# Hybrid encoder layer: the gate rows of the dense tokens multiplied on VectorE instead of GpSimd, with staging buffers on two sides of SBUF and five block loads placed in one of them

## The chip, the core and the metric

One core of a Trainium2 chip runs the whole program. The metric is device time in microseconds (us); lower is better. Engines are named as the profile names them: PE is TensorE (PEld its weight loads), DVE is VectorE, ACT is ScalarE, POOL is GpSimd, SP is SyncE. SPq, ACTq and POOLq are the DMA issues of an engine.

## What is computed

One encoder layer over 1024 tokens of width 1024 in float32: RMSNorm and an input projection, differential attention and a two-way retention, an output projection, then a product-key expert layer (PEER), and a last RMSNorm. The change lies in the expert layer, for one block of tokens:

```python
q = (xb @ w_query).reshape(tb, 8, 2, 128)
s = einsum('thpd,hpnd->thpn', q, sub_keys)           # 8 heads, two halves, 128 keys each
top_s, top_i = top_k(s, 16)
cand_s, cand_i = all sums and pairs of the two halves  # 16 x 16 a head
best_s, pos = top_k(cand_s, 16)
eid  = take_along_axis(cand_i, pos)                  # 16 of 16384 experts a head, 128 a token
gate = softmax(best_s)
act  = gelu(einsum('thkd,td->thk', take(expert_down, eid), xb))
out  = einsum('thk,thkd->td', gate * act, take(expert_up, eid))
```

## The kernel before

The 1024 tokens are eight tiles of 128. Three of them (set A) are done by *gathering*: POOL fetches, for each of the 128 chosen experts of every token, one row of 1024 numbers from `peer_u` (128 tokens at a time, one indirect DMA into a tile called `rows`, six buffers), DVE multiplies it with the token's vector `xng` and sums into `act` (L998), and later the same is done with `peer_v` into `gacc` (L1007). That is 768 indirect DMAs in all.

The other five tiles (set B, 640 tokens, the *dense tokens*) are done *densely*: all 16384 experts, in 128 blocks of 128. For a block `a`, PE makes the products of the block of `peer_u` (the input `ut[a]`) with the tokens, ACT applies Gelu (`hf`, 128 experts x 640 tokens), and DVE multiplies by a block of gates that is zero where an expert was not chosen (`gt`, L1070). The product goes, as high and low halves `hh` and `hl`, into a second matmul with the block of `peer_v` (`po`), and DVE adds it up in `acc` (L1104). Each float32 factor is split in two halves (`uh` by ACT at L1060, `ul` by DVE at L1061; `vh` and `vl` likewise), and three matmuls make one product.

The gates come from a stage of their own, **the gates stage** (L902 to L940). For each of the five dense tiles, `kT` and `gT` hold the chosen keys and gates, turned so that a token is a column. Then, for every group of four tokens (32 groups a tile, 160 in all):

- DVE makes the one-hot patterns of both key halves, `oh` (L920);
- ACT converts the second half into `bo` (L924);
- POOL multiplies the first half by the gates into `ao` (L927); in three of 32 groups ACT does it in four pieces (L930);
- PE multiplies `bo` with `ao`, which gives a token's 128 x 128 gates, `pg` (L933);
- ACT, or in 13 of 32 groups DVE, copies `pg` into the staging tile `stg` (L936, L938), 64 KB a partition, two buffers in one pool.

After a tile, eight stores of 1 MB move `stg` to the DRAM tensor `g_dr` (L940). The last tile's stores end the stage.

Then comes **the prologue** of the dense loop (L1122 to L1145): the first five blocks of `ut` are loaded into five tiles `first0` to `first4` (L1125, on ACT's queue) in a pool that lies where `stg` lay. For each of the five, ACT and DVE split it, PE makes its products into `hfirst`, and four gathers are taken. After that, the gates of the five blocks are loaded from `g_dr` into the same `first` tiles (L1141), `acc` is loaded with x (L1143), and the five multiplies L1070 on `first` follow; with the first of them the second matmuls can begin. The loop over blocks 5 to 127 takes 6 gathers a block.

What sets the order: the code is written for a tile framework that gives every engine its own list of instructions, by a scheduler, and adds the waits. Each engine, and each DMA queue, works through its list in order. A tile in a pool that takes the room of a closed pool waits for what last used that room.

Lines that the prediction's steps touch:

```python
stg = pg_.tile([P, P, P], F32, name="stg")                                   # L917
G.tensor_tensor(ao, oh[0], bc(gT[:, q:q + 4, None], [P, 4, P]), op=ALU.mult)  # L927
first = [pp.tile([P, DC * P], F32, name=f"first{a}") for a in range(FIRST)]   # L1123
nc.sync.dma_start(gts[a], g_dr[a])                                            # L1141
mark[0] = V.tensor_tensor(gt, gt, hf, op=ALU.mult).ins                        # L1070
```

Of the kernel before, what the change touches and what calls it, by code (L numbers as in the profile page):

```python
# [10 lines left out]
F32 = mybir.dt.float32  # L11
# [4 lines left out]
AF = mybir.ActivationFunctionType  # L16
ALU = mybir.AluOpType
# [4 lines left out]
P = 128  # L22
# [3 lines left out]
DC = D // P  # L26
# [14 lines left out]
FIRST = 5  # L41
# [13 lines left out]
def peer_layer(tc, ap, dbg=None):  # L55
    nc = tc.nc
# [3 lines left out]
    def bc(a, shape):  # L60
        return a.to_broadcast(shape)
# [15 lines left out]
    with ExitStack() as top:  # L77
# [821 lines left out]


        g_dr = dram.tile([P, P, wB], F32, name="g_dr")
        with ExitStack() as es:  # L902
            pc = es.enter_context(tc.tile_pool(name="gc", bufs=1))
            pw = es.enter_context(tc.tile_pool(name="gw", bufs=4))
            pg_ = es.enter_context(tc.tile_pool(name="gs", bufs=2))
            ps = es.enter_context(tc.tile_pool(name="gps", bufs=2, space=PSUM))
            iop = pc.tile([P, P, 4], BF16, name="iop")
            G.iota(iop, pattern=[[1, P], [0, 4]], base=0, channel_multiplier=0, allow_small_or_imprecise_dtypes=True)
            for i in range(nB):
                pT = ps.tile([P, 3, P], F32, name="gtp")  # L910
                for k in range(3):
                    PE.transpose(pT[:, k], selE[k][:, i].rearrange("p h k -> p (h k)"), ident)
                kT = pw.tile([P, 2, P], BF16, name="kT", bufs=1)
                V.tensor_copy(kT, pT[:, 0:2])
                gT = pw.tile([P, P], F32, name="gT", bufs=1)
                V.tensor_copy(gT, pT[:, 2])
                stg = pg_.tile([P, P, P], F32, name="stg")  # L917
                for q in range(0, P, 4):
                    o2 = pw.tile([P, 2, P, 4], BF16, name="oh")
                    V.tensor_tensor(o2, bc(iop[:, None], [P, 2, P, 4]), bc(kT[:, :, None, q:q + 4], [P, 2, P, 4]),  # L920
                                    op=ALU.is_equal)
                    oh = [o2[:, k].rearrange("p n t -> p t n") for k in range(2)]
                    bo = pw.tile([P, 4, P], F32, name="bo")
                    S.activation(bo, oh[1], AF.Copy)  # L924
                    ao = pw.tile([P, 4, P], F32, name="ao")
                    if q // 4 % 11:
                        G.tensor_tensor(ao, oh[0], bc(gT[:, q:q + 4, None], [P, 4, P]), op=ALU.mult)  # L927
                    else:
                        for j in range(4):
                            S.activation(ao[:, j], oh[0][:, j], AF.Copy, scale=gT[:, q + j:q + j + 1])  # L930
                    pg = ps.tile([P, 4, P], F32, name="pg", bufs=6)
                    for j in range(4):
                        PE.matmul(pg[:, j], bo[:, j], ao[:, j], start=True, stop=True)  # L933
                    dst, src = stg[:, :, q:q + 4], pg.rearrange("p t a -> p a t")
                    if q // 4 % 5 in (0, 2):
                        V.tensor_copy(dst, src)  # L936
                    else:
                        S.activation(dst, src, AF.Copy)  # L938
                for k in range(0, P, 16):
                    nc.sync.dma_start(g_dr.rearrange("a b t -> b a t")[:, k:k + 16, i * P:(i + 1) * P], stg[:, k:k + 16])  # L940
        early.close()


        gp = top.enter_context(tc.tile_pool(name="gp", bufs=1, side="right"))
        late = {}

        def tail(t, o):
# [65 lines left out]
        with ExitStack() as es:  # L1013
# [105 lines left out]
                        add(k, t)  # L1119


            with tc.tile_pool(name="pro", bufs=1, side="right") as pp:  # L1122
                first = [pp.tile([P, DC * P], F32, name=f"first{a}") for a in range(FIRST)]  # L1123
                for a, ur in enumerate(first):
                    S.dma_start(ur.rearrange("p (c e) -> p c e", e=P), ap["ut"][a])  # L1125
                load(FIRST)
                for a, ur in enumerate(first):
                    raw[a] = ur.rearrange("p (c e) -> p c e", e=P)
                    split_u(a)
                    ready[a] = ready[a], pp.tile([P, wB], F32, name=f"hfirst{a}")  # L1130
                    products(ps, ready[a][1], 2, *ready[a][0])
                    ready[a] = ready[a][1]
                    for _ in range(4):
                        next(gen)
                split_u(FIRST)
                load(FIRST + 1)
                values(0)
                values(1)
                for a, ur in enumerate(first):
                    gts[a] = ur[:, 0:wB]  # L1140
                    nc.sync.dma_start(gts[a], g_dr[a])  # L1141
                for t, o in zip(SETS["B"], acc):
                    nc.sync.dma_start(o, x1_dr[t])  # L1143
                for a in range(FIRST):
                    down(a)  # L1145
            for a in range(FIRST - 1, P):
                if a >= FIRST:
                    down(a)
# [70 lines left out]
```

## Time and profile before

| | |
|---|---|
| median of three runs | 3086.2 us (3084.46 to 3092.26) |
| the profiled run, its own time | 3082.46 us |
| span of the profiled run, first to last instruction | 3080.7 us |
| PE busy | 2830.5 us (92%) |
| DVE busy | 2556.9 us (83%) |
| POOL busy | 1678.9 us (54%) |
| ACT busy | 1055.1 us (34%) |
| moved by DMA | 770.87 MB, mean 250 GB/s |

The profile is of one execution. Its time and its span differ by 1.8 us, and it lies 3.7 us under the median. A share of busy time is an average over stages with different limits: the gates stage runs from 899 to 1124 us of the span, the prologue from 1124 to 1217, the loop from there to the end. The granted clock (PEclk) is TensorE's, as a share of full speed. A DMA share of 1.00 means that the core's 16 DMA engines were busy all the time.

### The profile page before, as it was taken

The page shows a single profiled execution, that of the slowest core. Times are in us where ns is not written, and L with a number is a line of the kernel's source. Part 1 is how long each engine was busy: PE and PEld are TensorE (multiplying, and loading weights), DVE is VectorE, ACT ScalarE, POOL GpSimd, SP SyncE. Part 2 cuts the span into 40 slices and gives each one's busy share as a digit, 9 for nine tenths or more (in the row PEclk, how much of TensorE's full clock was granted, in tenths as well). Part 3 has the DMA queues.
Part 4 walks back from the last instruction along what each step waited for, and adds up shares of the span by engine and source line. Part 5 has one row for each costly group of instructions (what it writes and reads, how often), then busy time and mean ns, then how long its engine had stood idle before and what let it go on. Part 6 is the DMA issues. An engine that isn't in the chain of part 4 may idle for free.

```text
span 3080.7 us, 44740 instructions
## 1 busy us (share of the span) xinstructions
PE 2830.5 (92%) x15999; PEld 2512.8 (82%) x15999; DVE 2556.9 (83%) x4867; ACT 1055.1 (34%) x1734; POOL 1678.9 (54%) x1335
## 2 busy tenths in 40 slices
PE   8999798898978846999999999999999999999998
PEld 6887577698976646988888888898999889989997
DVE  6466587579999955899999998988999889889997
ACT  4444566422237742222322222222222222222222
POOL 3422455245659954566656556566554466565551
PEclk9999999999999977999999999999999999999999
DMA  4334865353205688998898888999999899999994
GB/s 166 108 118 142 194 123 110 133 195 129 104 18 138 190 224 318 326 324 319 302 323 292 305 328 332 328 331 322 338 324 326 295 355 327 327 333 332 331 323 157
DMA packets 334832, 770.87 MB, mean 250 GB/s; under 512 B 26640, under 2 KB 133776, under 8 KB 334608
## 3 DMA queue, kind: packets, MB, share of 16 engines
q0 software_dynamic: 128128, 438.36, 41.2%
q1 hardware_dynamic: 203888, 324.72, 31.8%
q10 hardware_dynamic: 2592, 4.93, 0.5%
q8 instruction: 126, 2.06, 0.3%
q14 instruction: 98, 0.80, 0.1%
HBM read 678.70 MB, written 89.19 MB: 249 GB/s over the span
## 4 chain that ended last, share of the span: by engine, by line
PE 19%; issue 17%; DVE 16%; POOL 10%; DMA 7%; ACT 2%; SPq 1%; POOLq 0%; DVEq 0%; ACTq 0%
POOL rows L988 8%; DVE rows L998 3%; PE po L73 3%; PE po L75 3%; DVE gacc L1007 3%; PE po L74 3%; PE pa L73 3%; PE pa L74 3%; PE pa L75 3%; DVE oh L920 2%; DMA ur<-ut 2%; DMA rows<-peer_u,idx 1%; DVE acc L1104 1%; DMA vr<-peer_v 1%; POOL ao L927 1%
## 5 line engine op out<-in xcount | busy, mean ns | idle before, releaser
L988 POOL DMA_INDIRECT rows<-peer_u,idx x384 | 525.8, 1369 | 411.3 <-DVE act L998 248.0
L73 PE MATMUL pa<-nThB,uh 128*128 128x320 f32 x2048 | 636.4, 311 | 54.7 <-ACT uh L1060 39.8
L988 POOL DMA_INDIRECT rows<-peer_v,idx x384 | 469.6, 1223 | 393.8 <-DVE gacc L1007 326.5
L75 PE MATMUL pa<-nThB,ul 128*128 128x320 f32 x2048 | 633.8, 310 | 14.1 <-DVE ul L1061 14.1
L74 PE MATMUL pa<-nTlB,uh 128*128 128x320 f32 x2048 | 634.3, 310 | 0.0
L73 PE MATMUL po<-vh,hh 128*128 128x512 f32 x1280 | 511.0, 400 | 46.0 <-DVE acc L1104 40.8
L75 PE MATMUL po<-vh,hl 128*128 128x512 f32 x1280 | 505.2, 395 | 0.0
L74 PE MATMUL po<-vl,hh 128*128 128x512 f32 x1280 | 504.3, 394 | 0.0
L1007 DVE SCALAR_TENSOR_TENSOR gacc<-rows,act,gacc 128x1024 f32<-128x1024 f32 x384 | 493.3, 1285 | 6.2 <-DMA rows<-peer_v,idx 5.3
L998 DVE CUSTOM_DVE_ANT_0 rows<-rows,xng 128x1024 f32<-128x1024 f32 x384 | 459.3, 1226 | 34.9 <-DMA rows<-peer_u,idx 20.5
L73 PEld LDWEIGHTS pa<-nThB,uh 128*128 128x128 f32 x2048 | 387.7, 189 | 61.0 <-ACT uh L1060 40.0
L75 PEld LDWEIGHTS pa<-nThB,ul 128*128 128x128 f32 x2048 | 387.8, 189 | 15.8 <-DVE ul L1061 15.4
L74 PEld LDWEIGHTS pa<-nTlB,uh 128*128 128x128 f32 x2048 | 387.6, 189 | 4.4
L73 PEld LDWEIGHTS po<-vh,hh 128*128 128x128 f32 x1280 | 244.0, 191 | 103.6 <-DVE acc L1104 49.6
L1092 ACT ACTIVATE vh<-vr 128x512 fp32r<-128x512 f32 x256 | 160.5, 628 | 414.4 <-DMA vr<-peer_v 197.2
L75 PEld LDWEIGHTS po<-vh,hl 128*128 128x128 f32 x1280 | 243.8, 190 | 54.8 <-DVE hl L1077 0.4
L74 PEld LDWEIGHTS po<-vl,hh 128*128 128x128 f32 x1280 | 244.1, 191 | 46.6
L1060 ACT ACTIVATE uh<-ur 128x1024 fp32r<-128x1024 f32 x118 | 125.2, 1061 | 360.5 <-PE pa L74 226.6
L1061 DVE TENSOR_TENSOR ul<-ur,uh 128x1024 fp32r<-128x1024 f32 x118 | 144.3, 1223 | 106.3 <-ACT uh L1060 104.6
L933 PE MATMUL pg<-ao,bo 128*128 128x128 f32 x1280 | 182.2, 290 | 40.3 <-POOL ao L927 31.7
L927 POOL TENSOR_TENSOR ao<-oh,gT 128x512 f32<-128x512 bf16 x145 | 206.9, 1461 | 22.0 <-DVE oh L920 22.0
L868 ACT ACTIVATE hf<-pa 128x320 f32<-128x320 f32 x246 | 105.7, 430 | 328.9 <-PE pa L75 319.0
(346 smaller groups left out, 5415.0 us busy)
## 6 DMA issues: line engine op xcount, KB each, us to landing
vr<-peer_v SPq DMA_DIRECT2D x256, 256.0 KB, 6.0
ur<-ut SPq DMA_DIRECT2D x123, 512.0 KB, 5.7
g_dr<-stg SPq DMA_DIRECT2D x40, 1024.0 KB, 10.1
gt<-g_dr SPq DMA_DIRECT2D x123, 320.0 KB, 4.9
wr<-w_in SPq DMA_DIRECT2D x48, 512.0 KB, 3.8
wqr<-wq SPq DMA_DIRECT2D x16, 576.0 KB, 5.3
wq_dr<-wqh SPq DMA_DIRECT2D x16, 576.0 KB, 4.7
wq_dr<-wql SPq DMA_DIRECT2D x16, 576.0 KB, 3.3
```

What stands on the lines that cost most here:

```text
L73: PE.matmul(out, ah, bh, start=first, stop=False)
L74: PE.matmul(out, ah, bl, start=False, stop=False)
L75: PE.matmul(out, al, bh, start=False, stop=last)
L868: S.activation(hf[:, cs], pa, AF.Gelu)
L927: G.tensor_tensor(ao, oh[0], bc(gT[:, q:q + 4, None], [P, 4, P]), op=ALU.mult)
L933: PE.matmul(pg[:, j], bo[:, j], ao[:, j], start=True, stop=True)
L988: G.indirect_dma_start(out=u, out_offset=None, in_=table, in_offset=bass.IndirectOffsetOnAxis(ap=idx, axis=0))
L998: V.tensor_tensor_reduce(out=u, in0=u, in1=xn, scale=1.0, scalar=0.0, op0=ALU.mult, op1=ALU.add, accum_out=act[:, k:k + 1])
L1007: V.scalar_tensor_tensor(o, v, act[:, k:k + 1], o, op0=ALU.mult, op1=ALU.add)
L1060: S.activation(uh, ur, AF.Copy)
L1061: V.tensor_tensor(ul, ur, uh.bitcast(F32), op=ALU.subtract)
L1092: S.activation(vh, vr, AF.Copy)
```

## The change

In the gates stage, the product `ao` is made by DVE in all 160 groups; none is left on POOL, nor the pieces on ACT. All 160 copies of `pg` into `stg` are made by ACT. `stg` comes from two pools of one buffer each: even tiles on the left side of SBUF, odd tiles on the right side. The odd pool is closed after tile 3 (of 0 to 4). In its room the pool `gp` (of `rows`, `xng`, `act`, `gacc`) and the pool of the five `first` tiles are opened, and the five loads of `ut` are issued there, on SP's queue, ahead of the work of tile 4. The prologue is otherwise the same.

```diff
         g_dr = dram.tile([P, P, wB], F32, name="g_dr")
+        pros = ExitStack()
...
-            pg_ = es.enter_context(tc.tile_pool(name="gs", bufs=2))
+
+            odd = ExitStack()
+            pgs = [es.enter_context(tc.tile_pool(name="gs0", bufs=1)),
+                   odd.enter_context(tc.tile_pool(name="gs1", bufs=1, side="right"))]
...
-                stg = pg_.tile([P, P, P], F32, name="stg")
+                stg = pgs[i % 2].tile([P, P, P], F32, name="stg")
...
-                    if q // 4 % 11:
-                        G.tensor_tensor(ao, oh[0], bc(gT[:, q:q + 4, None], [P, 4, P]), op=ALU.mult)
-                    else:
-                        for j in range(4):
-                            S.activation(ao[:, j], oh[0][:, j], AF.Copy, scale=gT[:, q + j:q + j + 1])
+                    V.tensor_tensor(ao, oh[0], bc(gT[:, q:q + 4, None], [P, 4, P]), op=ALU.mult)
...
-                    if q // 4 % 5 in (0, 2):
-                        V.tensor_copy(dst, src)
-                    else:
-                        S.activation(dst, src, AF.Copy)
+                    S.activation(dst, src, AF.Copy)
                 for k in range(0, P, 16):
                     nc.sync.dma_start(g_dr.rearrange("a b t -> b a t")[:, k:k + 16, i * P:(i + 1) * P], stg[:, k:k + 16])
+                if i == (nB - 2 if nB % 2 else nB - 1):
+                    odd.close()
+                    gp = top.enter_context(tc.tile_pool(name="gp", bufs=1, side="right"))
+                    pp = pros.enter_context(tc.tile_pool(name="pro", bufs=1, side="right"))
+                    firsts = [pp.tile([P, DC * P], F32, name=f"first{a}") for a in range(FIRST)]
+                    for a, ur in enumerate(firsts):
+                        nc.sync.dma_start(ur.rearrange("p (c e) -> p c e", e=P), ap["ut"][a])
...
-        gp = top.enter_context(tc.tile_pool(name="gp", bufs=1, side="right"))
...
-            with tc.tile_pool(name="pro", bufs=1, side="right") as pp:
-                first = [pp.tile([P, DC * P], F32, name=f"first{a}") for a in range(FIRST)]
-                for a, ur in enumerate(first):
-                    S.dma_start(ur.rearrange("p (c e) -> p c e", e=P), ap["ut"][a])
...
+            for a in range(FIRST):
+                down(a)
+            pros.close()
```

The lines behind the change are numbered a little differently: L920 becomes L924, L940 becomes L937, L988 L991, L998 L1001, L1061 L1064, L1070 L1073. Below, the lists of instructions in the order in which each engine has them, without a time.

**Place 1, DVE at the start of the gates stage.** Before:

```order
L914 CAST kT<-gtp 128x256
L916 COPY gT<-gtp 128x128
L920 TENSOR_TENSOR oh<-iop,kT 128x1024 x5
L936 COPY stg<-pg 128x128x4
L920 TENSOR_TENSOR oh<-iop,kT 128x1024 x2
L936 COPY stg<-pg 128x128x4
```

Of the changed kernel:

```order
L918 CAST kT<-gtp 128x256
L920 COPY gT<-gtp 128x128
L924 TENSOR_TENSOR oh<-iop,kT 128x1024 x2
L930 TENSOR_TENSOR ao<-oh,gT 128x512 x2
L924 TENSOR_TENSOR oh<-iop,kT 128x1024 x2
L930 TENSOR_TENSOR ao<-oh,gT 128x512 x2
```

DVE's copies of `pg` are gone; two one-hots and two products alternate to the end of the tile, so each product stands one instruction behind its one-hot.

**Place 2, SP's queue around the stores of the last tile** (the x32 are tiles 0 to 3, the x8 tile 4). Before:

```order
L940 DMA g_dr<-stg 128x16x128 x32
L1044 DMA ur<-ut 128x1024
L940 DMA g_dr<-stg 128x16x128 x8
L1089 DMA vr<-peer_v 128x512 x2
L1143 DMA acc_10860<-x_dr_70 128x1024
...
L1053 DMA gt<-g_dr 128x640
L1004 DMA gacc<-x_dr_75 128x1024
L1141 DMA first_10868<-g_dr 128x640
```

Of the changed kernel:

```order
L937 DMA g_dr<-stg 128x16x128 x32
L944 DMA first_10402<-ut 128x1024
...
L1007 DMA gacc<-x_dr_75 128x1024
L1047 DMA ur<-ut 128x1024
L937 DMA g_dr<-stg 128x16x128 x8
L1092 DMA vr<-peer_v 128x512 x2
L1140 DMA first_10402<-g_dr 128x640
...
L1047 DMA ur<-ut 128x1024
L1142 DMA acc_10832<-x_dr_70 128x1024
```

The five loads of `ut` (before on ACT's queue, behind the stores) now stand on SP's queue between the stores of tile 3 and those of tile 4, and the five loads of `acc` stand behind the gate loads instead of ahead of them.

ACT towards the end of tile 4, of the changed kernel (before, the load of `xng` stood behind the first `uh<-first`):

```order
L935 ACTIVATE stg<-pg 128x128x4
L928 ACTIVATE bo<-oh 128x512
L997 DMA xng<-xn_dr_83 128x1024
L935 ACTIVATE stg<-pg 128x128x4 x2
L928 ACTIVATE bo<-oh 128x512 x4
L935 ACTIVATE stg<-pg 128x128x4 x2
```

The load of `xng` now stands in the middle of ACT's gate work: 25 of the 32 `bo` and 22 of the 32 copies of tile 4 stand ahead of it.

**Place 3, DVE and POOL at the start of the prologue.** DVE before (`ISA rows,act` is the gather's multiply and sum, L998):

```order
L936 COPY stg<-pg 128x128x4 x2
L1061 TENSOR_TENSOR ul<-first_10868,uh 128x1024
L1061 TENSOR_TENSOR ul<-first_10869,uh 128x1024
L998 ISA rows,act<-rows,xng 128x1024
L998 ISA act 128x1
```

Of the changed kernel:

```order
L930 TENSOR_TENSOR ao<-oh,gT 128x512 x2
L1001 ISA rows,act<-rows,xng 128x1024
L1001 ISA act 128x1
L1001 ISA rows,act<-rows,xng 128x1024
L1001 ISA act 128x1
L1001 ISA rows,act<-rows,xng 128x1024
L1001 ISA act 128x1
L1064 TENSOR_TENSOR ul<-first_10402,uh 128x1024
```

POOL before:

```order
L779 TENSOR_TENSOR eq<-eq,tif 128x1536
L927 TENSOR_TENSOR ao<-oh,gT 128x512 x145
L988 DMA rows<-peer_u,idx 128x1024 x26
L719 IOTA iot 128x256
L649 DMA wqh<-wq_dr 128x1152
```

Of the changed kernel:

```order
L779 TENSOR_TENSOR eq<-eq,tif 128x1536
L991 DMA rows<-peer_u,idx 128x1024 x24
L719 IOTA iot 128x256
L649 DMA wqh<-wq_dr 128x1152
L649 DMA wql<-wq_dr 128x1152
```

Three gather sums now stand ahead of the first `ul`, and POOL has nothing of the gates stage ahead of its first gathers; 24 of them stand ahead of the `IOTA`, where 26 stood.

## Rows read from the trace of the kernel before

**Rows 1.** The page: busy time of engines; PE in 40 slices; one DMA issue's landing
```profile
PE 2830.5 (92%) x15999; PEld 2512.8 (82%) x15999; DVE 2556.9 (83%) x4867; ACT 1055.1 (34%) x1734; POOL 1678.9 (54%) x1335
...
PE   8999798898978846999999999999999999999998
...
gt<-g_dr SPq DMA_DIRECT2D x123, 320.0 KB, 4.9
```
**Rows 2.** Stretches: us, busy (instructions) by engine, PEclk, DMA share, GB/s
```profile
899.00:1124.00 225.00, 183.64 (x1292) 158.29 (x1290) 219.00 (x235) 167.19 (x315) 206.94 (x145) 0.98 0.55 152
1124.00:1156.00 32.00, 0.00 (x0) 0.00 (x0) 0.00 (x0) 0.12 (x1) 0.00 (x0) 0.55 1.01 283
1156.00:1182.00 26.00, 16.89 (x98) 16.40 (x98) 2.97 (x3) 6.79 (x10) 6.17 (x6) 0.77 1.00 392
1182.00:1217.00 35.00, 23.99 (x142) 23.48 (x142) 28.95 (x47) 3.65 (x6) 27.28 (x19) 0.80 0.86 302
1217.00:1260.00 43.00, 37.76 (x198) 33.07 (x199) 34.24 (x52) 15.83 (x26) 14.79 (x14) 0.92 0.80 286
1300.00:2900.00 1600.00, 1546.70 (x8655) 1400.39 (x8654) 1446.32 (x2366) 427.27 (x683) 927.53 (x735) 0.99 0.91 323
```
**Rows 3.** Groups by line, 901 to 1123 us: count, busy, mean ns, idle before
```profile
L927 POOL TENSOR_TENSOR ao<-oh,gT 128x512 f32<-128x512 bf16 x145 | 206.9, 1461 | 22.0 <-DVE oh L920 22.0
...
L920 DVE TENSOR_TENSOR oh<-iop,kT 128x1024 bf16<-128x1024 bf16 x158 | 180.1, 1186 | 0.0
L936 DVE COPY stg<-pg 128x512 f32<-128x512 f32 x65 | 44.1, 678 | 1.6 <-PE pg L933 1.6
```
**Rows 4.** DVE in order of time, start of the gates stage: start, duration, instruction
```profile
899.01 0.42 DVE L914 CAST kT<-gtp 128x256 bf16<-128x256 f32 x1 [3.07 <-PE gtp L912]
899.36 0.28 DVE L916 COPY gT<-gtp 128x128 f32<-128x128 f32 x1
899.55 1.28 DVE L920 TENSOR_TENSOR oh<-iop,kT 128x1024 bf16<-128x1024 bf16 x2
...
900.15 1.29 DVE L920 TENSOR_TENSOR oh<-iop,kT 128x1024 bf16<-128x1024 bf16 x2
```
**Rows 5.** DVE in order of time, a float32 subtraction of 512 columns and its successor
```profile
1213.38 0.69 DVE L1093 TENSOR_TENSOR vl<-vr,vh 128x512 fp32r<-128x512 f32 x1
1213.99 1.22 DVE L998 CUSTOM_DVE_ANT_0 rows<-rows,xng 128x1024 f32<-128x1024 f32 x1
```
**Rows 6.** ACT in order of time, in the gates stage
```profile
947.34 0.58 ACT L938 ACTIVATE stg<-pg 128x512 f32<-128x512 f32 x1
947.82 2.38 ACT L924 ACTIVATE bo<-oh 128x512 f32<-128x512 bf16 x4
950.10 0.59 ACT L938 ACTIVATE stg<-pg 128x512 f32<-128x512 f32 x1
```
**Rows 7.** DMA queues, 1030 to 1125 us (two tiles' stores): packets, MB, share of 16 engines
```profile
q1 hardware_dynamic: 33030, 16.80, 64.2%
```
**Rows 8.** In order of time, the prologue; in brackets idle time before and what ended it
```profile
1156.72 5.11 ACTq L1125 DMA_DIRECT2D first<-ut  x5
...
1163.26 0.64 PE L73 MATMUL pa<-nThB,uh 128*128 128x320 f32 x1 [39.77 <-ACT uh L1060]
...
1181.48 1.23 DVE L998 CUSTOM_DVE_ANT_0 rows<-rows,xng 128x1024 f32<-128x1024 f32 x1 [14.15 <-DMA xng<-xn_dr]
...
1192.87 0.64 PE L75 MATMUL pa<-nThB,ul 128*128 128x320 f32 x1 [12.72 <-DVE ul L1061]
...
1216.87 2.29 DVE L1070 TENSOR_TENSOR first<-first,hfirst 128x640 f32<-128x640 f32 x3
```
**Rows 9.** DMA queues, 1156 to 1217 us: packets, MB, share of 16 engines
```profile
q0 software_dynamic: 3299, 12.04, 54.9%
q1 hardware_dynamic: 1954, 5.51, 23.9%
q10 hardware_dynamic: 864, 3.15, 13.0%
```

More of the change, by code (lines that the diff above doesn't have):

```diff
@@ L1119, in up @@
                         add(k, t)
-            with tc.tile_pool(name="pro", bufs=1, side="right") as pp:
-                first = [pp.tile([P, DC * P], F32, name=f"first{a}") for a in range(FIRST)]
-                for a, ur in enumerate(first):
-                    S.dma_start(ur.rearrange("p (c e) -> p c e", e=P), ap["ut"][a])
[L1126 to L1145, printed above, removed]
+            load(FIRST)
+            for a, ur in enumerate(firsts):
+                raw[a] = ur.rearrange("p (c e) -> p c e", e=P)
+                split_u(a)
+                ready[a] = ready[a], pp.tile([P, wB], F32, name=f"hfirst{a}")
+                products(ps, ready[a][1], 2, *ready[a][0])
+                ready[a] = ready[a][1]
+                for _ in range(4):
+                    next(gen)
+            split_u(FIRST)
+            load(FIRST + 1)
+            values(0)
+            values(1)
+            for a, ur in enumerate(firsts):
+                gts[a] = ur[:, 0:wB]
+                nc.sync.dma_start(gts[a], g_dr[a])
+            for t, o in zip(SETS["B"], acc):
+                nc.sync.dma_start(o, x1_dr[t])
+            for a in range(FIRST):
+                down(a)
+            pros.close()
             for a in range(FIRST - 1, P):
```

## The prediction

> **What bounds the kernel now.** First the share of each engine and PE's 40 slices [rows 1]: PE is busy 92% of the span, its low digits in the early stages and where gates stage and prologue lie. Then the stretches [rows 2]. In the loop (1300 to 2900) PE is busy 1546.7 of 1600 us, DVE 1446.3, the DMA engines 0.91: PE leads, so whatever lets the loop start earlier moves the end by as much. What matters is the 318 us between 899 and 1217, in which PE does not lead.
>
> In the gates stage (225 us, 160 groups, 1.41 us each) DVE is busy 219.0 us and POOL 206.9: both are full, and they get in each other's way. The one-hot `oh` follows its predecessor after 0.60 us in the first groups, before POOL has a product to make [rows 4]; over the stage it takes 1.186 us [rows 3].
>
> Between 1124 and 1156 no engine works; the DMA engines do, at 1.01 [rows 2]: the last tile's stores. The five `first` loads need the room of `stg` and are issued at 1156.7; PE waits 39.8 us. Then DVE waits 14.2 us for `xng`, and with it PE 12.7 us for `ul` [rows 8]. The DMA engines are at 1.00 up to 1182 and at 0.86 up to 1217 [rows 2]. So transfers pace the prologue. At 1216.9 stands the first multiply of the five blocks by their gates (L1070 on `first`, "the first multiply"), behind 20 gather sums on DVE.
>
> **The gates stage after.** POOL's 145 products and ACT's 60 pieces go, DVE's 65 copies (44.1 us, [rows 3]) go to ACT, 160 products come to DVE. With POOL still, a one-hot should cost its 0.60. The product on DVE is in no row: 512 columns, one operand bfloat16, one float32. From below, the one-hot's pace (1024 bfloat16 columns in 0.60) would make it 0.30; from above, POOL's own 1.461 [rows 3]. I take 0.61, the step of a float32 subtraction of 512 columns [rows 5], since the result and an operand are float32. A group then takes DVE 1.21 us. ACT steps 2.28/4 = 0.57 for a `bo` and 0.48 for a copy [rows 6], 1.05: it stays under DVE. PE was fed at 1.41 with busy 183.6 of 225 [rows 2] and its pulses overlap; I cost it nothing. A tile: 32 x 1.21 + 0.54 for `kT` and `gT` [rows 4] = 39.3; five 196.3. From 899.0 DVE ends at 1095.3, the last copy about 2 us later at **1097, 27 us earlier** than 1124. At the lower price ACT would bind, 32 x 1.05 + 0.54 = 34.1 a tile, and save 26 us more; the upper price is a rival.
>
> The Trainium skill, "VectorE: DVE Perf Modes", section "The DRAIN you can't avoid", says that a Vector instruction does not start until the pipe behind its predecessor has emptied. Here two one-hots last 1.28 us together and start 0.60 apart [rows 4], so they overlap by 0.08; by the rule the group would cost full durations, and the forecast would be that of rival 2.
>
> **The prologue after.** It can't start before tile 3's stores have left the odd room. DVE ends tile 3 at 899.0 + 4 x 39.3 = 1056.2; with some 3 us for what stands behind it the stores begin at 1059. Two tiles' stores (16.80 MB) took 0.642 x 95 = 61.0 us of all engines [rows 7], 30.5 a tile, so they are out at **1090**. From there gathers, `xng` and the five loads run, 7 us ahead of the end of tile 4. ACT's issue of `xng` has the same wait, and behind it are queued ten copies and seven `bo` of tile 4. ACT would come to it at about 1056 + 24 x 1.21 + 1.5 = 1087, so it stands still for 3 us, and needs 10 x 0.48 + 7 x 0.57 = 8.8 us for the rest: ready at 1099 instead of 1097. DVE is four one-hots ahead (four buffers) and is not held. It costs up to 2 us, more if the stores are late, and only PE's first products notice. On SP the last tile's stores stand behind the loads, but begin only with the end of the tile anyway.
>
> What must be moved between 1090 and the first multiply, in time of all 16 engines [rows 7, 9]: `first` and `xng` 3.15 MB, 0.130 x 61 = 7.9; `gacc` and one `ur`, 1.05 MB at the second queue's 5.51 MB in 14.6 us, 2.8; the stores 30.5; 20 to 24 gathers at 1.46 us (12.04 MB in 33.5 us, 0.524 MB each) 29.2 to 35.0; two `vr` and a gate block 2.3. **Sum 72.7 to 78.5 us.** The same account for before, from 1156.7: 7.9 + 14.6 + 33.5 = 56.0 us of work in the 60.2 us up to the first multiply, 93% full. So after: 1163 at the least; 1172 with 24 gathers and all but the stores at 93%. One gate block lands 4.9 us after its issue [rows 1]: the first multiply at 1168 to 1177 instead of 1216.9, **40 to 49 us earlier**, 45 in the middle.
>
> PE's work hides under this: `ul` of block 0 stands behind three gather sums and so behind `xng`, which shares the engines with 7.9 + 6 x 1.46 us of others and lands between 1095 and 1108; take `ul` at 1104. A block costs PE 48 x 23.99/142 = 8.1 us at the mixed clock of 1182 to 1217 [rows 2], five 40: 1144. PE then stands again for 25 us and its clock falls (0.55 in 1124 to 1156, the lower of 1.2 and 2.4 GHz for most of it [rows 2]); it did so before, so nothing is added.
>
> Behind the first multiply a debt is left: `acc` and four gate blocks, 3.93 MB, 10.4 us of transfers that before were done by then. From 1217 to 1260 the engines were free for 0.20 x 43 = 8.6 us [rows 2]; 2 us remain. **Gain 45 - 2 = 43 us**; the profiled run's 3082.5 becomes 3039.5, the median 3086.2 becomes **3043**.
>
> **Rivals.**
>
> 1. *The engines pace the prologue*: stores and gathers don't lengthen each other. For it: gathers and loads together moved 392 GB/s up to 1182, stores alone 283 [rows 2]. Against it: both filled the engines. First multiply 1145, gain 72 - 2: **3016**. The Trainium skill, "DMA: Bandwidth & Descriptors", section "Queues, rings and completion order", says that each engine takes turns between queues packet by packet. Stores have packets of 16.80 MB/33030 = 0.5 KB, gathers of 3.6 KB [rows 7, 9]; by the rule stores come last and this rival falls. No row shows the two together.
>
> 2. *DVE's instructions don't overlap*: a group costs 0.677 + 0.69 = 1.37 us (1.28 - 0.60 = 0.68 for the one-hot alone). For it: each product waits for a DVE result, which nothing in this stage did before. Against it: an instruction stands between. Gates 160 x 1.37 + 3 = 222 us, saving 3; tile 3 ends at 1077, stores out at 1111, first multiply 1111 + 78 + 5 = 1194, gain 23 - 2: **3065**.
>
> 3. *Mixing costs bandwidth*: gathers beside stores go at the stores' 16.80/61 = 0.275 MB per us, 1.9 instead of 1.46, 24 x 0.44 = 10.6 us, and the debt of 10.4 is paid in full. Gain 40 - 10.6 - 10.4 = 19: **3067**.
>
> 4. *Slower: the product costs DVE what it cost POOL*, 1.46 us, because of its mixed types and its operand read in steps of four. A group 2.06, a tile 66.5; tile 3 done at 1168, stores out at 1199, tile 4 done at 1233. Behind it 30.5 of stores, 18 gathers 26.3, 2.3 and 4.9: first multiply 1297, 80 us later: **3166**. It turns slower from where four tiles last 43 us more, 50 us a tile, a product of 0.95 us. Against it: the float32 subtraction of the same size, with two operands too, takes 0.69 [rows 5].
>
> 5. *The room is not free early*, and the loads come behind the last stores as now: the gates' 27 us alone, **3059**. Against it: place 2 of the order.
>
> **How the numbers follow.** Forecast (first multiply 1168 to 1177, loop moved as a whole) 0.60, 3036 to 3050. Rival 1: 0.12. Rival 2: 0.10. Rival 3: 0.10. Rival 4: 0.05. Rival 5: 0.03. A measurement tells 0.3%, 9 us. Forecast, rivals 1 and 5 and four fifths of 2 and 3 are faster by more, 0.91; what is left of 2 and 3 and a mild form of 4 lies within, 0.05; slower 0.04. The range, 3018 to 3066, leaves out rival 4, most of 3 and half of 1.
>
> **What the profile would show.** Gates stage 198 us, `oh` near 0.68 and `ao` near 0.69 without idle time between; copies on ACT 0.59. First `first` load near 1090, PE's first product near 1100 instead of 1163, the engines of the DMA full up to about 1170, first multiply there, and a loop of the same length behind it. Wrong would be: a one-hot that stays at 0.9 without POOL, a product over 0.9, a first multiply before 1155 or after 1185, or PE's loop longer than before.

## The result and the profile after

The changed kernel takes 3035.6 us (median of 4 runs, 3031.4 to 3039.0) against 3085.3 us of the kernel before timed beside it (3082.0 to 3092.3): a ratio of 0.9836, 95% interval 0.982 to 0.9852. That is 49.7 us or 1.6% faster; 3043 with a range of 3018 to 3066 was forecast. Its profiled execution took 3036.5 us, its span 3034.7. The page after, the rows that answer to [rows 1]: totals of PE, PEld, DVE, ACT and POOL; PE in 40 slices.

```profile
PE 2836.0 (93%) x15999; PEld 2516.7 (83%) x15999; DVE 2539.4 (84%) x4962; ACT 1069.3 (35%) x1739; POOL 1471.2 (48%) x1190
...
PE   8999789899979986999898998999999999999998
```

PE works as much as before (2836 against 2830 us) in a span 46 us shorter, and POOL has lost 208 us, the 145 products. The stretches after, answering to [rows 2]: us, busy time (instructions) of PE, PEld, DVE, ACT and POOL, PEclk, DMA share, GB/s.

```profile
903.00:1108.00 205.00, 185.19 (x1293) 158.99 (x1291) 198.19 (x334) 183.53 (x321) 7.90 (x7) 0.98 0.66 191
...
1108.00:1146.00 38.00, 33.76 (x216) 33.23 (x216) 27.40 (x41) 7.73 (x12) 24.32 (x17) 0.96 1.06 397
1146.00:1162.00 16.00, 0.00 (x0) 0.00 (x0) 0.00 (x0) 0.00 (x0) 0.00 (x0) 0.58 1.07 306
...
1250.00:2850.00 1600.00, 1546.97 (x8641) 1399.61 (x8640) 1443.38 (x2361) 424.75 (x680) 927.46 (x735) 0.98 0.91 323
```

Three things are to be seen. The gates stage lasts 205 us instead of 225. The stretch in which no engine computes and only transfers run lay **between** the stage and PE's products and lasted 38.0 us (1124.13, the end of ACT's last copy, to 1162.15, its next instruction; the row of 32 us is cut inside it). It lies **behind** the products now and lasts 20.6 us (1143.8 to 1164.39; the row of 16 us is cut inside it), because the products run while the stores drain. And 1600 us of the loop hold 1547.0 us of PE, as before (1546.7): it was moved, not shortened. The gates stage by groups (count, busy us, mean ns, idle before), answering to [rows 3], and DVE in order of time at its start, answering to [rows 4]:

```profile
L930 DVE TENSOR_TENSOR ao<-oh,gT 128x512 f32<-128x512 bf16 x160 | 104.1, 698 | 3.2 <-PE pg L933 2.2 <-issue 1.0
L924 DVE TENSOR_TENSOR oh<-iop,kT 128x1024 bf16<-128x1024 bf16 x158 | 102.6, 697 | 2.4 <-ACT bo L928 2.4
L935 ACT ACTIVATE stg<-pg 128x512 f32<-128x512 f32 x159 | 94.6, 596 | 19.8 <-PE pg L933 9.6 <-issue 6.0
```

```profile
903.16 0.42 DVE L918 CAST kT<-gtp 128x256 bf16<-128x256 f32 x1 [3.29 <-PE gtp L916]
...
903.70 1.28 DVE L924 TENSOR_TENSOR oh<-iop,kT 128x1024 bf16<-128x1024 bf16 x2
904.90 1.29 DVE L930 TENSOR_TENSOR ao<-oh,gT 128x512 f32<-128x512 bf16 x2
```

Two one-hots, then two products, a pair from 903.70 to 904.90: 0.60 us a step for either. The one-hot that took 1.186 us on average beside POOL takes 0.697. This run came to the stage 4.15 us later than the run of before (its first one-hot at 903.70 against 899.55), ahead of everything that was changed; two more executions of the same kernel came there at 903.64 and 907.14. So I count from the first one-hot where two runs are compared.

### The profile page after: what moved, and what is told of

Its sections match the earlier page's. It is cut to its first block, busy times and chain, and to the rows that moved or that the text cites. A ratio compares the mean times of both kernels' runs of the same rounds, so it can differ in the third digit from the quotient of the medians.

```text
span 3034.7 us, 44517 instructions
## 1 busy us (share of the span) xinstructions
PE 2836.0 (93%) x15999; PEld 2516.7 (83%) x15999; DVE 2539.4 (84%) x4962; ACT 1069.3 (35%) x1739; POOL 1471.2 (48%) x1190
## 4 chain that ended last, share of the span: by engine, by line
PE 21%; issue 16%; DVE 14%; POOL 9%; DMA 6%; SPq 2%; ACT 2%; POOLq 0%; DVEq 0%; ACTq 0%
POOL rows L991 8%; DVE gacc L1010 4%; PE po L73 3%; PE po L75 3%; PE po L74 3%; PE pa L73 3%; PE pa L74 3%; PE pa L75 3%; DVE rows L1001 3%; SPq L937 2%; DMA ur<-ut 2%; DMA vr<-peer_v 2%; PE pg L933 2%; DVE acc L1107 1%; DVE ao L930 1%
## 5 line engine op out<-in xcount | busy, mean ns | idle before, releaser
L991 POOL DMA_INDIRECT rows<-peer_u,idx x384 | 523.2, 1362 | 554.8 <-DVE act L1001 227.5
L991 POOL DMA_INDIRECT rows<-peer_v,idx x384 | 470.8, 1226 | 396.0 <-DVE gacc L1010 329.8
L73 PE MATMUL po<-vh,hh 128*128 128x512 f32 x1280 | 512.0, 401 | 39.3 <-DVE acc L1107 38.9
L1001 DVE CUSTOM_DVE_ANT_0 rows<-rows,xng 128x1024 f32<-128x1024 f32 x384 | 460.2, 1228 | 21.4 <-DMA rows<-peer_u,idx 19.9
L75 PEld LDWEIGHTS po<-vh,hl 128*128 128x128 f32 x1280 | 243.9, 191 | 54.7
L1064 DVE TENSOR_TENSOR ul<-ur,uh 128x1024 fp32r<-128x1024 f32 x118 | 144.7, 1226 | 100.5 <-ACT uh L1063 87.1
L1096 DVE TENSOR_TENSOR vl<-vr,vh 128x512 fp32r<-128x512 f32 x256 | 177.7, 694 | 44.6 <-ACT vh L1095 43.7
L1107 DVE TENSOR_TENSOR acc<-po,acc 128x512 f32<-128x512 f32 x320 | 204.8, 686 | 4.1 <-PE po L75 4.1
```

Source lines behind the costliest of these rows:

```text
L73: PE.matmul(out, ah, bh, start=first, stop=False)
L75: PE.matmul(out, al, bh, start=False, stop=last)
L991: G.indirect_dma_start(out=u, out_offset=None, in_=table, in_offset=bass.IndirectOffsetOnAxis(ap=idx, axis=0))
L1001: V.tensor_tensor_reduce(out=u, in0=u, in1=xn, scale=1.0, scalar=0.0, op0=ALU.mult, op1=ALU.add, accum_out=act[:, k:k + 1])
L1064: V.tensor_tensor(ul, ur, uh.bitcast(F32), op=ALU.subtract)
L1096: V.tensor_tensor(vl, vr, vh.bitcast(F32), op=ALU.subtract)
```

## The prologue after

SP's queue in order of time (start, duration of the issue), for what stood on ACT and SP in [rows 8]:

```profile
1062.00 24.43 SPq L937 DMA_DIRECT2D g_dr<-stg  x8
1094.04 2.64 SPq L944 DMA_DIRECT2D first<-ut  x5
1096.73 0.58 SPq L1007 DMA_DIRECT2D gacc<-x_dr  x1
1107.37 0.33 SPq L1047 DMA_DIRECT2D ur<-ut  x1
1107.96 48.86 SPq L937 DMA_DIRECT2D g_dr<-stg  x8
1156.86 4.31 SPq L1092 DMA_DIRECT2D vr<-peer_v  x2
1161.27 2.66 SPq L1140 DMA_DIRECT2D first<-g_dr  x5
```

The five loads start at 1094.04, in the middle of tile 4, 190.3 us behind the first one-hot (before: 1156.72, 257.2 behind it). The last tile's eight stores keep SP issuing for 48.9 us; those of tile 3, with nothing beside them, took 24.4. DVE over the same time (in brackets idle time and what ended it):

```profile
1109.62 1.22 DVE L1064 TENSOR_TENSOR ul<-first,uh 128x1024 fp32r<-128x1024 f32 x1
...
1139.43 1.23 DVE L1001 CUSTOM_DVE_ANT_0 rows<-rows,xng 128x1024 f32<-128x1024 f32 x1
...
1165.05 0.69 DVE L1096 TENSOR_TENSOR vl<-vr,vh 128x512 fp32r<-128x512 f32 x1 [24.38 <-ACT vh L1095]
...
1166.61 0.82 DVE L1073 TENSOR_TENSOR first<-first,hfirst 128x640 f32<-128x640 f32 x1
```

The first multiply stands at 1166.61 instead of 1216.87. The gather sums end at 1140.7 and PE's products at 1143.8; DVE then stands for 24.4 us with nothing to do but wait for `vr` and the gate blocks, which stand behind the stores on SP's queue. The DMA queues from the loads' issue to the first multiply, 1094 to 1166 us (packets, MB, share of 16 engines), answering to [rows 9]:

```profile
q1 hardware_dynamic: 18029, 13.11, 57.4%
q0 software_dynamic: 3456, 12.58, 43.1%
q10 hardware_dynamic: 144, 0.52, 1.9%
```

The shares add to 1.02 over 72 us: 26.3 MB, with a gap only in the first two us (a share of 0.39 from 1094 to 1096). By these rows transfers pace the prologue, as they did before; the run with fewer gathers below tests it.

## The experiments

Everything below is counted from the first one-hot of the gates stage in the profiled execution: "loads" is the issue of the first `first` load, "multiply" the first multiply of a block by its gates, "loop" the time from the first multiply into `po` to the start of the last sum into `acc`. Medians are of 4 runs of the kernel (5 for the last pair), ratios against the kernel before on the same chip in the same series. Its median was 3085.3 us in the first and 3089.5 to 3095.3 in the others, so the ratios compare better than the medians.

| kernel | loads us | multiply us | loop us | median us | ratio (95%) |
|---|---|---|---|---|---|
| before | 257.2 | 317.3 | 1847.5 | 3085.3 | 1 |
| after | 190.3 | 262.9 | 1851.8 | 3035.6 | 0.9836 (0.982 to 0.9852) |
| gates only | 229.8 | 289.8 | 1852.4 | 3064.1 | 0.9909 (0.9892 to 0.9925) |
| early loads only | 214.0 | 288.6 | 1862.6 | 3061.9 | 0.9897 (0.988 to 0.9913) |
| after, `xng` on SP | 189.7 | 261.5 | 1860.1 | 3042.2 | 0.9847 (0.983 to 0.9863) |
| after, one gather a block | 190.3 | 246.4 | 1860.6 | 3035.1 | 0.9827 (0.9807 to 0.9846) |
| one gather, RATE 6.12 | 190.2 | 246.2 | 1875.1 | 3039.6 | 0.9821 (0.9783 to 0.986) |
| the same, `xng` on SP | 190.2 | 246.1 | 1873.8 | 3043.8 | 0.9839 (0.9799 to 0.9878) |
| no gather, RATE 6.165 | 190.2 | 243.9 | 1878.2 | 3038.4 | 0.9825 (0.979 to 0.986) |
| after again | 189.8 | 262.6 | 1854.8 | 3039.0 | 0.983 (0.9795 to 0.9864) |
| after, RATE 5.88 | 190.5 | 263.4 | 1833.6 | 3024.2 | 0.9787 (0.9756 to 0.9817) |
| after, RATE 5.8 | 189.7 | 263.6 | 1846.2 | 3047.3 | 0.9842 (0.9822 to 0.9861) |
| RATE 5.88, second time | 190.3 | 262.9 | 1830.3 | 3024.3 | 0.9792 (0.977 to 0.9813) |
| after, beside it | 189.7 | 263.2 | 1861.2 | 3038.3 | 0.9833 (0.9811 to 0.9855) |

**The two parts apart.** First the gate part alone: the kernel before, with the product on DVE and all copies on ACT.

```
-                    if q // 4 % 11:
-                        G.tensor_tensor(ao, oh[0], ...)
-                    else: ...
+                    V.tensor_tensor(ao, oh[0], ...)
...
-                    if q // 4 % 5 in (0, 2):
-                        V.tensor_copy(dst, src)
-                    else: ...
+                    S.activation(dst, src, AF.Copy)
```

> The kernel before with the gates stage alone changed: products on VectorE, copies on ScalarE; one pool of two staging buffers, loads of the first five blocks behind the stores as before. Theory (the two parts of the change are worth about the same and add up, the stage by its work on VectorE, the prologue by its transfers): a tile 39.1 us instead of 44.5, no hold in the last tile, since the load of xng stands behind the gates again; gates stage about 197 us instead of 225, and the prologue as before (40 us of standing PE, first multiply some 93 us after the end of the stage): 24 to 28 us faster than before, 3057 to 3062. Rival a (all of the gain lies in the stage, the early loads only hide what the stores' transfers take anyway): 3036 to 3042. Rival b (a shorter stage only makes the prologue wait longer for transfers): 3075 to 3086.

Measured: 3064.1 us, 28.6 below the kernel before beside it, and the multiply 27.5 us earlier than before. DVE's groups in its gates stage (910 to 1100 us):

```profile
L920 DVE TENSOR_TENSOR oh<-iop,kT 128x1024 bf16<-128x1024 bf16 x157 | 100.5, 678 | 0.0
L926 DVE TENSOR_TENSOR ao<-oh,gT 128x512 f32<-128x512 bf16 x156 | 99.8, 678 | 0.0
```

No idle time, and both at the length of a lone instruction. Next the other part alone: the changed kernel with the old division of products and copies (the reverse of the diff above).

> The changed kernel with the old gates stage: products on GpSimd (three groups in 32 on ScalarE), 13 of 32 copies on VectorE; the staging buffers on two sides and the five early loads are kept. Theory (transfers pace the prologue): tile 3's stores out at about 1112, the five loads done before the stage ends at 1124, GpSimd's gathers not before 1123; then stores 30.5, 20 to 24 gathers at 1.46 us and 2.3 us of others, 62 to 68 us: first multiply near 1190 instead of 1216.9, 22 to 28 us faster than before, 3058 to 3064. Rival a (the gain is in the stage): 3075 to 3086. Rival c (without the early gathers the loads bring nothing, since GpSimd's list holds them back): 3070 to 3080.

Measured: 3061.9 us, 30.8 below the kernel before beside it, the multiply 28.7 us earlier. The one-hot beside POOL is back at its old price (901 to 1118 us):

```profile
L931 POOL TENSOR_TENSOR ao<-oh,gT 128x512 f32<-128x512 bf16 x143 | 204.5, 1464 | 22.6 <-DVE oh L924 22.6
L924 DVE TENSOR_TENSOR oh<-iop,kT 128x1024 bf16<-128x1024 bf16 x156 | 178.6, 1191 | 0.0
```

What follows: 27.5 + 28.7 = 56.2 us against 54.4 of both together, so the parts add up at the multiply, and each is worth about half (by the times 0.9% and 1.0%, against 1.6 to 1.7% of both). The early loads gain less than the 43.2 us by which they start earlier (214.0 against 257.2), since from their issue to the multiply it takes 74.6 us instead of 60.1: the last tile's stores now lie inside that time. The one-hot's 678 against 1191 ns shows that its length beside POOL was contention; at the start of the stage before, where POOL has no product yet, it takes 0.68 too [rows 4]. The Trainium skill, "SBUF — State Buffer", section "Who interferes with whom", says that a Vector instruction with two inputs in SBUF contends with a GpSimd instruction that reads SBUF, at a pair of ports that the two share; these rows agree in direction. POOL paid as well: the last product of the stage before, beside which DVE has no instruction, takes 1.03 us against the mean of 1.46.

```profile
1121.24 1.03 POOL L927 TENSOR_TENSOR ao<-oh,gT 128x512 f32<-128x512 bf16 x1
```

**The hold at `xng`.** ACT and then DVE in order of time in tile 4 of the changed kernel:

```profile
1088.87 0.68 ACT L928 ACTIVATE bo<-oh 128x512 f32<-128x512 bf16 x1
1094.06 0.35 ACTq L997 DMA_DIRECT2D xng<-xn_dr  x1
1094.45 1.08 ACT L935 ACTIVATE stg<-pg 128x512 f32<-128x512 f32 x2 [4.90 <-issue]
```

```profile
1092.45 1.30 DVE L930 TENSOR_TENSOR ao<-oh,gT 128x512 f32<-128x512 bf16 x2
1096.12 1.29 DVE L924 TENSOR_TENSOR oh<-iop,kT 128x1024 bf16<-128x1024 bf16 x2 [2.37 <-ACT bo L928]
```

ACT stands for 4.9 us at the issue of `xng`, which waits for tile 3's stores; DVE loses 5.6 us in four pieces (2.37, 0.84, 1.01, 1.39) and PE 5.4 in one. Is that on the path? The edit takes the issue off ACT:

```
-                (nc.sync if i else S).dma_start(xn, xn_dr[t])
+                nc.sync.dma_start(xn, xn_dr[t])
```

> The changed kernel with the first load of xng on SP's queue, behind the five block loads, instead of on ScalarE's. In the changed kernel ScalarE stood still for 4.9 us at that load, waiting for tile 3's stores, VectorE was held for 5.6 us and the last tile took 48.5 us instead of 39. Theory (transfers pace): the last tile ends some 7 us earlier, but the DMA engines are full from 1098 on either way and stood only about 2.6 us between 1090 and 1098: first multiply 0 to 3 us earlier, total within 3 us of the changed kernel. Rival (the hold is on the path that sets the end, since the last stores start behind it): first multiply and total 6 to 8 us earlier, 3028 to 3030.

Measured: the last product of the stage starts 194 us behind the first one-hot instead of 200, and the multiply moves by 1.4 us, from 262.9 to 261.5; the time, 3042.2 us, is no better. The 6 us are real and hidden: the last tile's stores are issued 6.9 us earlier, but their issue lasts 55.1 us instead of 48.9 and ends 0.7 us earlier.

**How many bytes stand ahead of the multiply.** In the prologue each of the five blocks' products is followed by four steps of the gather generator; one instead of four:

```
-                for _ in range(4):
+                for _ in range(1):
                     next(gen)
```

> The changed kernel with one gather for each of the five first blocks in the prologue instead of four; the 15 others come later, at the end of the kernel (23 instead of 8 gather sums behind the last multiply by the gates). Theory (transfers pace the prologue): 9 instead of 24 gathers before the first multiply, 15 x 1.46 = 22 us of transfers less; PE's products of the five blocks (to about 1144) then come close: first multiply at 1145 to 1152 instead of 1166.6, and what is gained there is mostly lost at the end, where 15 gathers at 1.2 to 1.5 us stand alone: total 3030 to 3042. Rival 1 (stores and gathers do not lengthen each other; the stores' own time or the engines pace): first multiply stays at 1160 to 1167, and the total is 12 to 22 us longer, 3048 to 3058.

Measured: 3035.1 us, the multiply 16.5 us earlier with 15 gathers fewer, 1.10 us each. The DMA queues between the loads' issue and the multiply (1089 to 1144.6 us):

```profile
q1 hardware_dynamic: 18094, 13.25, 78.1%
q0 software_dynamic: 1296, 4.72, 21.1%
q10 hardware_dynamic: 144, 0.52, 2.4%
```

18.5 MB in 56.1 us, the engines again at 1.02: bytes out, time out. That shows what paces the prologue, and with it the forecast's rival that stores and gathers don't lengthen each other falls. The gain is lost further on: 23 gather sums instead of 8 stand behind the last gate multiply, and the span ends 20.6 us behind the last sum into `acc` instead of 10.2. Against the rest stands a loop of 1860.6 us instead of 1851.8, which is within the spread of the changed kernel's own loops.

**Can the loop take the gathers?** RATE is the number of gather steps that the program puts beside one block of the loop. At 6.12 instead of 6.0, 14 of the 15 gathers that left the prologue go into the loop:

```
-RATE = 6.0
+RATE = 6.12
```

Two relatives went with it: the same with `xng` on SP, and one with no gather step between the products (`range(0)`, RATE 6.165).

> The kernel of the run with one gather a block in the prologue, and RATE 6.12 in place of 6.0, so that 9 gather sums instead of 23 stand behind the last gate multiply. Theory (transfers pace the prologue, the multiplies on TensorE pace the loop, and the gathers have room in it): the first multiply stays where the one-gather run had it, about 247 us behind the gates stage's start, the some 20 us of lone gather sums at the end shrink to about 8, and the time is 3015 to 3026 us, 0.973 to 0.979 of the kernel before. Rival (the transfers of the loop are full too, and a gather moved out of the prologue costs its 1.46 us there again): the loop takes the 14 gathers with about 20 us, and the time stays at 3032 to 3040 us.

> The run with one gather a block and RATE 6.12, with the first row tile (xng) issued on SP instead of ACT. Theory: with 15 gathers fewer the transfers no longer cover all of the hold at the end of the gates stage, since the products on TensorE end only some 10 us ahead of the first multiply; taking the hold away brings 0 to 4 us: 3012 to 3025 us. Rival (the hold is on the path as soon as the gathers are out of the way): 6 to 8 us, 3008 to 3018 us.

> No gather step between the five blocks' products, RATE 6.165, so that 8 gather sums stand behind the last gate multiply; the first row tile is then issued only behind the gates stage, so that nothing holds ACT at its end. Theory: five gathers fewer than the one-gather run at 1.46 us and the row tile's 1.3 us put the first multiply some 8 us earlier, at about 238 us behind the stage's start, near the end of TensorE's products (about 235): 3006 to 3020 us. Rival (the loop's transfers are full): what is saved ahead comes back in the loop, 3030 to 3042 us.

Measured: 3039.6, 3043.8 and 3038.4 us. The theory of all three was wrong, by 19 to 25 us from the middle of its range: the multiply came where it was expected in the first two (246.2 and 246.1), and the loop became 1873.8 to 1878.2 us long. The rivals of the first and the third, by which the loop pays for what leaves the prologue, had the time right (3032 to 3040 and 3030 to 3042). Nor did `xng` on SP gain anything here, where the multiply stays (246.1 against 246.2); the rival there expected 6 to 8 us. In the third the multiply came at 243.9 instead of 238: the row tile stayed on ACT in tile 4 (ACT again idle 4.82 us there), and the bytes ahead of the multiply only fell from 18.5 to 17.5 MB, not by five gathers, because other loads moved up, a row tile of the expert work among them. What PE waits for most between 1300 and 1900 us (us in total, times, longest), at RATE 6.12 with one gather a block:

```profile
PE e L73 <- DMA wqh<-wq_dr: 20.7, 5, 6.3
PE po L73 <- DVE acc L1107: 15.2, 10, 3.8
PE pa L75 <- DVE ul L1064: 6.2, 1, 6.2
```

and in the changed kernel:

```profile
PE po L73 <- DVE acc L1107: 26.6, 12, 6.4
PE e L73 <- DMA wqh<-wq_dr: 7.9, 2, 7.2
```

The weights `wqh` of the expert work that runs in this part of the loop come later, and so does `ul`. The loop isn't paced by PE alone in this part. That the loop's transfers are full, as the rivals had it, is not shown: the DMA share of the whole loop is 0.89 to 0.90 in all of these. So the opposite step, the changed kernel with fewer gathers in the loop:

```
-RATE = 6.0
+RATE = 5.88
```

> The changed kernel with RATE 5.88 in place of 6.0: 15 gather sums fewer among the multiplies on the other engines' queues, 23 instead of 8 behind the last gate multiply. If a gather sum inside the loop costs the loop about 1 us each, as the step from RATE 6.0 to 6.12 says (1860.6 to 1875.0 us between the first multiply into po and the last sum into acc, for 14 gathers), the loop becomes 12 to 18 us shorter than the changed kernel's 1851.8 (1834 to 1840 us), the 15 stand alone behind it with about 18 us, and the time stays within 6 us: 3030 to 3042 us. Rival (TensorE alone paces the loop, and what was lost at 6.12 was only a later arrival of the weights wqh): the loop keeps 1848 to 1855 us, and the time rises by the 18 us, to 3050 to 3057 us.

Measured: **3024.2 us**, better than either side expected, with a loop of 1833.6 us, as the theory had it. The stretch from 1300 to 1900 us, of the changed kernel and then of RATE 5.88 (columns as in the stretches above):

```profile
1300.00:1900.00 600.00, 559.28 (x3149) 504.96 (x3148) 548.05 (x1111) 159.17 (x252) 359.81 (x295) 0.96 0.87 310
```

```profile
1300.00:1900.00 600.00, 573.04 (x3278) 521.79 (x3278) 560.26 (x1107) 165.38 (x262) 379.11 (x302) 0.98 0.90 318
```

PE stands 27 us instead of 41. The 15 sums more at the end did not stand alone with 18 us: part of them fits between the last sums into `acc`, and the span ends 20.6 us behind the last of these instead of 10.2. Does that go on?

> The changed kernel with RATE 5.8: 33 gather sums behind the last gate multiply, 10 more than at 5.88. Theory (a gather sum costs the loop about 1.2 us, and some 20 of those left behind fit beside the last two blocks' multiplies): the loop, 1833.6 us at 5.88, becomes 10 to 12 us shorter again, and the 10 sums stand alone behind it with 12 to 15 us: 3022 to 3032 us, no better than 3024. Rival (the sums left behind still find room beside the last multiplies): 3008 to 3016 us.

Measured: 3047.3 us; both sides wrong. The 33 sums left behind end the span 33.8 us after the last sum into `acc`, and the loop, 1846.2 us, is longer than at 5.88 though it holds ten sums fewer. Its profiled execution took 3054.8 us, 7.5 over the median. Over the loop PE stands for 49.4 us in it, against 46.4 at 5.88 and 56.9 in the changed kernel, and is busy for 1796.8, 1787.3 and 1794.9 us with the same 10002 matmuls. Of the 12.6 us between the loops of 5.8 and 5.88, 3.1 are waiting and 9.5 are more time at work, at a mean granted clock over the span of 0.968 against 0.973. Ten sums fewer saved no waiting, so the theory "a gather sum costs the loop 1 us" falls: RATE moves every gather and every step of the expert work against the blocks, and how they meet decides what PE waits for. Which meeting costs what at 5.8 stays open. Whether 5.88 was an accident of its series is told by two pairs: the changed kernel in the series of 6.12, and 5.88 and the changed kernel side by side on one chip.

> The changed kernel itself, beside the other three on the same chip: 3031 to 3040 us, 0.982 to 0.985 of the kernel before, with the first multiply 261 to 266 us behind the gates stage's start. Nothing is told apart by it but the run-to-run variation of the stages ahead of the change, which each theory leaves at some 10 us.

> RATE 5.88 beside the changed kernel on one chip, since the two were timed apart so far (3024.2 against 3035.6 and 3039.0 us) and RATE 5.8 did not continue the series. If the order at 5.88 suits the loop, 3018 to 3028 us again with the loop from the first multiply into po to the last sum into acc at 1830 to 1838 us; if the single call was lucky, 3030 to 3040 us and a loop of 1845 to 1855 us.

> The changed kernel beside it: 3031 to 3040 us by either reading, with the loop at 1850 to 1856 us and the first multiply 261 to 266 us behind the gates stage's start.

Measured: 3039.0 us for the changed kernel in the series of 6.12, where the others had 3038 to 3044; then 3024.3 us (3020.6 to 3027.0) at 5.88 against 3038.3 (3032.9 to 3048.2) of the changed kernel, loops 1830.3 and 1861.2 us. The profiled execution of the changed kernel took 3048.2 us here, 10 over its median; PE stands for 45.3 and 58.3 us of the two loops, so 13 of the 31 us are waiting. The version with RATE 5.88 beats both kernels: 0.9792 of the time before, 11 to 14 us below the changed kernel. Whether the kernel before would gain as much at 5.88 was not run, so this gain can't be put down to the change.

## Why the prediction was right, step by step

- **The gates stage.** Forecast 1.21 us a group and 39.3 a tile; measured 1.20 and 39.1 in the tiles that nothing holds. The product on DVE, which no row of before showed, was taken at the step of a float32 subtraction, 0.61, out of bounds of 0.30 and 1.46; it is 0.60. The rival with 1.46 and the one in which DVE's instructions don't overlap fall by the rows above: durations of 0.70, starts 0.60 apart. The rule of the Trainium skill that was weighed there ("VectorE: DVE Perf Modes", "The DRAIN you can't avoid") would have cost 0.17 us a group more than was measured; the section's own pointer, that an instruction which isn't held starts earlier, is what these rows show.
- **The loads.** Forecast 1090, 191 us behind the stage's start; measured 190.3.
- **The hold at `xng`.** That ACT would stand was right; that DVE would not be held was wrong, and the size was off. Forecast 3 us of ACT, up to 2 us in the end and "DVE is not held"; measured 4.9 us of ACT, 5.6 of DVE, and the last copy of the stage at 1107.9, 204 us behind the first one-hot instead of 198 to 200. The one-hots ahead do not cover the stop: DVE went on to 1093.8, with four more one-hots and four products, and then waited 2.37 us for a `bo`. It cost the multiply 1.4 us only, as the experiment with `xng` on SP shows, because the transfers lasted as long either way.
- **PE's products.** Forecast 1104 to 1144; measured 1110.9 (the first `ul` product) to 1143.8. A later start was made up by a higher granted clock, 0.96 over 1108 to 1146 instead of the 0.80 of [rows 2].
- **The transfers.** This is the term that was mis-sized. Forecast 72.7 to 78.5 us of transfers with 20 to 24 gathers, up to 82 with a part of them at 93%, and 4.9 for the last landing: 78 to 87 us from the loads to the multiply, at 1168 to 1177. Measured 72.6 us, at 1166.6, or 1162.5 on the clock of the run before. 24 gathers took 0.431 x 72 = 31.0 us of all engines, 1.29 each instead of 1.46, and the engines were at 1.02, so that the allowance of 93% was not needed. From the issue of the gate blocks to the multiply it took 5.3 us (1161.27 to 1166.61), the two `vl` in front of it included.
- **Mixing.** The rival by which gathers beside stores would go at the stores' pace falls: 397 GB/s from 1108 to 1146 against 306 for the stores alone behind it. The Trainium skill, "DMA: Bandwidth & Descriptors", section "Queues, rings and completion order", which the forecast weighed against rival 1, has the engines take turns packet by packet. The stores did come last, but the turns were not one for one as this profile counts packets: from 1108 to 1146, 2991 packets (10.88 MB) of gathers went with 6796 (4.16 MB) on the stores' queue. The issue of the stores took 48.9 us beside gathers and 31.6 with one gather a block.
- **The room.** Rival 5, the loads behind the last stores, falls by the loads at 1094.04; its case is that of the gate part alone, 3064.1 us against the 3059 that it priced.
- **The loop and the debt.** Forecast 2 us of debt; the loop is 4.3 us longer in the profiled pair (1851.8 against 1847.5), and three runs of the changed kernel spread from 1851.8 to 1861.2, so that a debt of this size can't be told from the loop's own spread.

By the rows of the profiled pair: the multiply 50.3 us earlier, 1.0 lost up to `po`, 4.3 in the loop, 1.0 gained at the end, 46.0 us of span. The forecast said 45 and 2, 43. The later arrival at the stage hides 4.15 us of this: counted from the first one-hot, the multiply is 54.4 us earlier and the end 50.2, and the medians differ by 49.7. So the forecast was right by its mechanism, with two errors of size that partly cancel: the multiply came 9 us earlier than forecast, counted so, and 4.3 us instead of 2 were lost behind it.

## What to carry to other kernels

When transfers pace a stretch, count its bytes from the moment the first of them may start to the instruction that waits for the last, and price a step by whether it moves that moment or those bytes; engine time saved inside it, such as the 6 us at `xng`, was worth nothing here. An instruction of an engine that is slow beside GpSimd should be priced once by its start-to-start time where GpSimd is idle: the one-hot's first groups gave the forecast's 0.60 us, its mean of 1.19 did not. And after a change in front of a loop whose side work is spread by a rate, the rate is worth measuring anew in both directions, since the loop's own length answered to it with anything from 1830 to 1878 us, and not in proportion.

## What was not expected of the hardware

Gathers beside stores moved 397 GB/s (1108 to 1146 us) on one core, as much as loads and gathers did without stores (392, [rows 2]), and stores alone 283 to 306. So mixing in packets of 0.5 KB did not lower the rate here, although more than a quarter of the bytes were on the stores' queue. It fits that 15 gathers fewer gave back 1.10 us each, not the 1.29 that their share of the engines says; why, no run shows. A stop of 4.9 us on ACT, whose own instructions filled only 184 of 205 us, was enough to stop PE for 5.4 us, and the clock granted to PE afterwards was the lower level, 1.2 of 2.4 GHz, for some microseconds:

```profile
1094.00:1098.00 4.00, 1.86 (x8) 1.86 (x9) 1.29 (x2) 3.30 (x6) 2.13 (x3) 0.50 0.66 233
1098.00:1102.00 4.00, 4.00 (x26) 4.00 (x26) 2.74 (x5) 2.47 (x5) 3.08 (x4) 0.66 1.02 412
```

(the changed kernel's stretches around the stop; PEclk is the number ahead of the DMA share).
